# A sixth raw-weight buffer taken from the DMA scratch: one decoder layer in split float32 on one core

## The chip, the cores and the metric

The kernel runs on one core of one Trainium2 chip. The metric is device time in microseconds of one execution; three executions of the kernel before were timed, and the median counts. The profile is of one execution, taken by the hardware profiler.

## The reference

One decoder layer on 512 tokens of width 1024. Two token mixers run side by side on the normed input, are merged by sigmoid gates, and are followed by a squared-ReLU MLP.

```
h = rms_norm(x); proj = h @ w_in        # split into u, q, six key/value parts, gates
y_pool = pool_mixer(u)                  # causal means over 2, 4, 8, 16 tokens, then a small matmul
y_nsa  = nsa_mixer(q, kc, vc, ks, vs, kw, vw)   # compressed, selected and window attention, 16 heads
merged = g_a * (y_pool @ w_proj_pool) + g_b * (y_nsa @ w_proj_nsa)
x = x + merged @ w_out
x = x + square(relu(rms_norm(x) @ w_ff1)) @ w_ff2
return rms_norm(x)
```

All weights are float32 and each is read from HBM once or a few times.

## The kernel before, in words

**Weights.** Every matrix product is made of three products of split operands: a weight block of 128 x 1024 numbers (512 KB) is loaded into a raw tile, ScalarE copies it to a high part (`wh`), VectorE subtracts that from the raw block to get the low part (`wl`), and TensorE multiplies. One such pair of steps is called a conversion here. The blocks to be loaded stand in the list `LD`, in the order in which they are converted; `emit_load` (line 278) issues the next one on SyncE's queue (line 297). Before the change there are `RAW = 4` raw tiles, used in turn, so load number i has to wait until block i - 4 is converted. Four loads are issued at the start, and each conversion ends with one `emit_load`, so that in the program's order, too, loads run four conversions ahead.

**Converted parts.** They go into a ring of two places (`wh`, `wl`), or for the compression MLP and some gate blocks into one place called `wkt`. A block can only be converted when TensorE has finished with the one that had its place.

**Stages.** The stage up to attention ends at `N1` (number 37 in `LD`): compression keys (ck), selected keys (ks), the four pool groups (u0 to u3), the compression MLP (wk0 to wk3, wv0 to wv3), values (V0 to V2), the first queries (q0, q1, q2), the pool weights (wpool, number 19), and two groups of gate products in a seven-product Strassen form (A11, S3, S1 and so on; the first block of the first group is number 20). Then come attention, with the rest of the queries and gate columns as filler (`FILL2`), the NSA projection (pn0 to pn7), the output projection and the MLP, again in Strassen form. From `MLP0` (number 68) on tiles are handed back by name (`give_back`): `spare` collects them, and a seventh-product tile called raw5 joins there, so that five tiles are in use in the MLP.

**Sums of weights.** Some Strassen blocks are sums of two weight blocks. `make_sum` copies one block from HBM to HBM (tiles `S_g`, `S_o`, `S`; line 335, SyncE's queue), and `add_sum` adds the other with an accumulating DMA issued from GpSimd (line 343). Both are tied to the number of the load that has just been issued, and loads `raw<-S` read the result.

**Other traffic on SyncE's queue.** Each rotary embedding (`rope`) swaps halves with four small DMAs (line 882, `rs<-rx`, 64 KB each), on which VectorE's multiplications at line 899 wait.

**Order.** Instructions of an engine run in the order that a planner fixed when the program was built, from its own estimates of times; `tc.issue_after` (here `behind`) ties an instruction behind another of the same engine, and `tc.high_priority` moves one forward.

Of the kernel before, what the change touches and what calls it, by code (L numbers as in the profile page):

```python
# [62 lines left out]
def trunk(ctx: ExitStack, tc: tile.TileContext, A, out):  # L63
    nc = tc.nc
# [35 lines left out]
        return f[:, 1024 * i:1024 * i + 1024].rearrange("p (k t) -> p k t", k=4)  # L100

    WL, LD = [], []
    RAW = 4

    def add_w(key, ap):
        WL.append((key, len(LD)))
# [63 lines left out]
    for k in P1 + FILL2:  # L170
# [11 lines left out]
        if k == P1[-1]:  # L182
            N1 = len(LD)
# [85 lines left out]
    dest = {}  # L269

    raws, hls = {}, {}
    st = {"load": 0, "prep": 0, "use": 0, "kept": 0, "pairs": 0, "sums": 0}
    spare, slots_hl = [], []
    held, begun = {}, deque()

# [2 lines left out]
    def emit_load():  # L278

        i = st["load"]  # L280
        if i >= len(LD):
            return False
        segs = LD[i]
        a = segs[0][0].shape[1]
        b = sum(s.shape[2] for s, _ in segs)
        assert a * b <= 1024
        if not by_name() or st["kept"] < RAW:
            st["kept"] += by_name()
            t = wp.tile([128, 1024], F32, tag="raw", bufs=RAW, name=f"raw{i}")
        elif spare:  # L290
            t = spare.pop(0)
        else:
            return False
        st["load"] += 1
        v = t[:, :a * b].rearrange("p (a b) -> p a b", a=a)
        for s, o in segs:
            began[0] = nc.sync.dma_start(v[:, :, o:o + s.shape[2]], s)
        raws[i] = (t, a, b)
        for _ in range(sums_after(i)):
            make_sum(began[0])  # L300
        while i in EARLY[1:] and begun:
            add_sum()
        if (26 <= i < N1 and len(begun) > 1) or i >= N1 + len(FILL2) + 4 and (len(begun) > 2 or begun and st["sums"] == len(jobs)):
            add_sum()
        while i == MLP0 + 6 and len(begun) > 2:
            add_sum()
        return True
# [3 lines left out]
    def sums_after(i):  # L311

        if i < MLP0:
            return i in EARLY or i in (26, 27, 33, 35, 36) or N1 + 3 <= i < N1 + len(FILL2) or i == MLP0 - 2
        if i < MLP0 + 12:
            return {3: 1, 6: 4}.get(i - MLP0, 0)
        return (i - MLP0) % 3 == 0

    def by_name():

        return st["load"] >= MLP0

    def give_back(*tiles):
        spare.extend(tiles)
        while spare and by_name() and emit_load():
            pass

    def make_sum(load):

        if st["sums"] < len(jobs):  # L330
            to, q, _ = jobs[st["sums"]]
            while any(q is jobs[n][0] for n in begun):
                add_sum()
            with tc.issue_after(load.ins):
                nc.sync.dma_start(to, q)
            begun.append(st["sums"])
            st["sums"] += 1

    def add_sum(behind=None):

        to, _, q = jobs[begun.popleft()]
        with tc.issue_after(behind.ins) if behind else nullcontext():
            POOL.dma_start(to, q, accum_op=ALU.add)  # L343
# [28 lines left out]
    def group_steps(i):  # L372

        key, at = WL[i]
        if i in PLUS:
            while st["load"] <= PLUS[i]:
                assert emit_load()
            t = raws.pop(PLUS[i])[0]
            DVE.tensor_tensor(t, t, held[key], op=ALU.add)
            give_back(held.pop(key))  # L380
            yield
        elif isinstance(at, str):
            t = held.pop(key)
        else:
            while st["load"] <= at:
                assert emit_load()
            t = raws.pop(at)[0]
# [20 lines left out]
    kept = {}  # L408
# [52 lines left out]
    def wo_steps(i):  # L461
# [17 lines left out]
        if o in ("A12", "S2"):  # L479
# [3 lines left out]
            kept.pop("S2")  # L483
        if st["load"] > RAW + MLP0:
            give_back(t)
        else:
            emit_load()
            if st["kept"] == RAW:
                give_back()
# [4 lines left out]
    def emit_prep_half():  # L494
# [38 lines left out]
        raws.pop(at)  # L533
        if st["load"] > RAW + MLP0:
            give_back(t)
        else:
            emit_load()
            if st["kept"] == RAW:
                give_back()
# [246 lines left out]
    def behind(made):  # L786
        return tc.issue_after(made.ins)
# [22 lines left out]
    def evac0(i, after=None, root=None):  # L810
        sl = slice(128 * i, 128 * i + 128)
        for a in range(2):
            ks = slice(4 * a, 4 * a + 4)
            with behind(root) if root else nullcontext():
                r = ACT.activation(hT[0][:, ks, sl], trs[i][a], AF.Copy)
            with behind(after) if after else nullcontext():
                v = DVE.tensor_tensor(hT[1][:, ks, sl], trs[i][a], hT[0][:, ks, sl].bitcast(F32), op=ALU.subtract)
        for a in range(2 if i > 1 else 0):
            c = 128 * (i - 2)
            ACT.activation(quarter(MAf, 2 * a + 1)[:, :, c:c + 128], trs[i][a], AF.Copy)  # L820
        return r, v
# [7 lines left out]
    r, _ = evac0(1)  # L829
# [21 lines left out]
    made = []  # L851
# [5 lines left out]
        DVE.tensor_copy(identR, ident)  # L857
    c0.close()
    made0 = list(made)
    with behind(made[0]):  # L860
        ACT.activation(tick, rr[3][:, 1:2], AF.Sigmoid)

# [77 lines left out]
    with ExitStack() as c1:  # L940
# [254 lines left out]
        for k in P1[2:]:  # L1195
            i = int(k[-1]) if k[-1].isdigit() else None
# [533 lines left out]
    with ExitStack() as c3:  # L1730
# [21 lines left out]
        class Merged:  # L1752

            made = {b: [m[:, 4 * i:4 * i + 4, 256 * j:256 * j + 256] for m in mT]
                    for b, i, j in (("11", 0, 0), ("21", 1, 0), ("22", 1, 1))}
# [329 lines left out]
```

## Time and profile before

| what | value |
|---|---|
| three runs, us | 772.26, 770.54, 770.27 |
| median, us | 770.54 |
| profiled execution, span of the page, us | 767.4 |
| profiled execution's own time | not listed apart from its span; the median lies 3.1 us above the span |
| TensorE (PE) busy | 756.7 us, 99% |
| VectorE, ScalarE, GpSimd busy | 87%, 67%, 24% |
| mean busy share of the DMA engines by slice | from 0.1 to 1.0 |

The span runs from the first to the last instruction. Most executions of one kernel agree within 0.3%.

### The profile page before, as it was taken

How to read it: one execution, taken by the hardware profiler on the slowest of the kernel's cores; microseconds unless marked ns; L12 is line 12 of the kernel's file. 1: busy time of each engine (PE TensorE's matmuls, PEld its weight loads, DVE VectorE, ACT ScalarE, POOL GpSimd, SP SyncE). 2: the span in 40 equal slices, each digit the busy share in tenths (PEclk: the TensorE clock that was granted, in tenths of full speed). 3: DMA queues.
4: the chain of work that ended last, by engine and by line, in shares of the span. 5: the costliest groups of instructions: out<-in, count | busy, mean ns of one | idle time of the engine just before them, and what ended most of it. 6: DMA issues, size and time to landing. Idle time of an engine off the chain costs nothing.

```text
span 767.4 us, 13409 instructions
## 1 busy us (share of the span) xinstructions
PE 756.7 (99%) x4757; PEld 675.9 (88%) x4757; DVE 666.4 (87%) x1279; ACT 511.1 (67%) x977; POOL 184.2 (24%) x264
## 2 busy tenths in 40 slices
PE   9999999999999999999999999999999999999996
PEld 7889889888888888888889899989998999889985
DVE  7897999548988889989689689997989788978897
ACT  7766655328878888898745576954774477447754
POOL 4001010117746766574000200111111110111001
PEclk9999999999999999999999999999999999999999
DMA  9559993983051833371357965989998999799942
GB/s 308 165 143 266 251 230 108 257 214 115 15 176 52 158 56 70 56 138 60 116 186 220 324 111 185 287 219 299 310 259 222 314 303 257 215 325 294 293 171 110
DMA packets 119886, 150.76 MB, mean 196 GB/s; under 512 B 5782, under 2 KB 92346, under 8 KB 119611
## 3 DMA queue, kind: packets, MB, share of 16 engines
q1 hardware_dynamic: 98250, 122.90, 48.3%
q0 software_dynamic: 21280, 26.22, 22.8%
q8 instruction: 38, 0.62, 0.3%
q10 hardware_dynamic: 288, 0.79, 0.3%
q14 instruction: 30, 0.24, 0.1%
HBM read 145.16 MB, written 54.53 MB: 260 GB/s over the span
## 4 chain that ended last, share of the span: by engine, by line
PE 84%; DVE 9%; ACT 2%; DMA 2%; issue 1%; POOL 1%; SPq 0%; DVEq 0%; ACTq 0%; POOLq 0%
PE psB L638 20%; PE psB L1698 18%; PE psF L568 16%; PE psB L568 6%; PE psV L638 5%; PE psS L1378 4%; PE psT L1440 4%; PE psO L1474 4%; PE psB L1647 3%; DMA raw<-w_in 2%; PE psF L700 1%; DVE wl L527 1%; DVE PT L1456 1%; DVE P L1400 1%; DVE wkt L527 1%
## 5 line engine op out<-in xcount | busy, mean ns | idle before, releaser
L343 POOL DMA_DIRECT2D S<-w_ff x44 | 49.0, 1113 | 351.3 <-DMA S<-w_ff 290.3
L568 PE MATMUL psF<-R,wh 128*128 128x512 f32 x384 | 124.6, 400 | 0.0
L390 ACT ACTIVATE wh<-raw 128x1024 fp32r<-128x1024 f32 x73 | 77.1, 1058 | 70.0 <-PE psB L638 24.0
L1423 POOL TENSOR_SCALAR P<-P,sm,GT 128x128 f32<-128x128 f32 (+3 forms) x128 | 85.5, 724 | 68.8 <-DVE sm L1420 36.1
L395 DVE TENSOR_TENSOR wl<-raw,wh 128x1024 fp32r<-128x1024 f32 x73 | 88.9, 1219 | 12.7 <-ACT wh L390 12.2
L568 PEld LDWEIGHTS psF<-R,wh 128*128 128x128 f32 x384 | 68.8, 188 | 11.4 <-issue 0.2
L1410 ACT ACTIVATE P<-P,sm 128x128 f32<-128x128 f32 (+3 forms) x128 | 71.0, 557 | 9.9 <-DVE sm L1400 6.2
L568 PE MATMUL psF<-R,wl 128*128 128x512 f32 x192 | 75.5, 393 | 0.0
L524 ACT ACTIVATE wh<-raw 128x512 fp32r<-128x512 f32 (+1 forms) x76 | 45.1, 616 | 32.9 <-PE psF L568 21.2
L1400 DVE CUSTOM_DVE_ANT_0 P<-psS,cst 128x128 f32<-128x128 f32 (+3 forms) x128 | 59.3, 482 | 4.9 <-PE psT L1440 2.7
L390 ACT ACTIVATE w3h<-raw 128x1024 fp32r<-128x1024 f32 x37 | 39.2, 1059 | 34.0 <-PE psB L638 12.6
L527 DVE TENSOR_TENSOR wl<-raw,wh 128x512 fp32r<-128x512 f32 (+1 forms) x74 | 51.5, 707 | 9.2 <-ACT wh L524 8.9
L1451 ACT ACTIVATE PT<-psT 128x512 fp32r<-128x512 f32 (+2 forms) x96 | 49.0, 520 | 13.9 <-PE psT L1440 13.0
L1456 DVE TENSOR_TENSOR PT<-psT,PT 128x512 fp32r<-128x512 f32 (+2 forms) x96 | 56.2, 591 | 1.5 <-ACT PT L1451 1.3
L1440 PE MATMUL psT<-ident,P 128*128 128x128 f32 x320 | 50.1, 273 | 0.6 <-POOL rx L899 0.4
L395 DVE TENSOR_TENSOR w3l<-raw,w3h 128x1024 fp32r<-128x1024 f32 x37 | 45.1, 1220 | 4.7 <-ACT w3h L390 4.5
L1474 PE MATMUL psO<-PT,VV 128*128 128x256 f32 x320 | 48.5, 286 | 0.0
L1440 PEld LDWEIGHTS psT<-ident,P 128*128 128x128 f32 x320 | 39.6, 140 | 9.4 <-POOL rx L899 0.8
L638 PE MATMUL psB<-R,wh 128*128 128x256 f32 x336 | 46.3, 279 | 0.0
L1474 PEld LDWEIGHTS psO<-PT,VV 128*128 128x128 f32 x320 | 42.2, 188 | 1.3 <-ACT PT L1451 0.3
L638 PEld LDWEIGHTS psB<-R,wh 128*128 128x128 f32 x336 | 42.5, 188 | 0.2
L568 PEld LDWEIGHTS psF<-R,wl 128*128 128x128 f32 x192 | 36.0, 188 | 7.5
(442 smaller groups left out, 2083.7 us busy)
## 6 DMA issues: line engine op xcount, KB each, us to landing
raw<-w_ff SPq DMA_DIRECT2D x54, 512.0 KB, 6.2
S<-w_ff POOLq DMA_DIRECT2D x44, 512.0 KB, 8.2
raw<-S SPq DMA_DIRECT2D x44, 512.0 KB, 5.3
S<-w_ff SPq DMA_DIRECT2D x32, 512.0 KB, 7.3
raw<-w_in SPq DMA_DIRECT2D x31, 512.0 KB, 4.7
S<-S SPq DMA_DIRECT2D x12, 512.0 KB, 6.7
raw<-w_proj_nsa SPq DMA_DIRECT2D x8, 512.0 KB, 4.1
x<-x SPq DMA_DIRECT2D x7, 512.0 KB, 6.5
```

What stands on the lines that cost most here:

```text
L390: ACT.activation(h, t, AF.Copy)
L395: DVE.tensor_tensor(l, t, h.bitcast(F32), op=ALU.subtract)
L527: eng.tensor_tensor(l[:, sl], t[:, sl], h[:, sl].bitcast(F32), op=ALU.subtract)
L568: PE.matmul(ps, a, b, start=first and j == 0, stop=last and j == n - 1, skip_group_check=True)
L638: PE.matmul(out, w[u][:, k, 128 * f:128 * f + 128], moving[v][:, k, :], **kw)
L1400: DVE.tensor_tensor_reduce(out=P[:, o:o + n].rearrange("p (a c) -> p a c", c=128), in0=s, in1=m, scale=1.0, scalar=3e38, op0=ALU.add, op1= ...
L1410: last_exp[:] = [ACT.activation(c, c, AF.Exp, bias=sm[:, 0, e:e + 1], scale=-1.0, accum_out=sm[:, 1, e:e + 1])]
L1423: r = POOL.tensor_scalar(P[:, o:o + n], P[:, o:o + n], sm[:, 2, e:e + 1], GT[:, qb, c + e:c + e + 1], op0=ALU.mult, op1=ALU.mult)
L1440: PE.transpose(pt[:, 128 * j:128 * j + 128], P[:, 128 * j:128 * j + 128], ident)
L1456: return DVE.tensor_tensor(dL, src, dH.bitcast(F32), op=ALU.subtract)
L1474: PE.matmul(ps[:, qb % 2, :, :], VV[:, k, b, g, :], t[:, j, :, :], start=False, stop=last and j == len(kbs) - 1 and t is tL, skip_group_ch ...
L1698: PE.matmul(ps[f], self.Y.of(y)[u][:, 2 * g + k, 128 * f:128 * f + 128], w[v][:, k, :], start=first and g == k == u == v == 0, stop=g == k ...
```

## The change

The scratch that the DMA descriptors of GpSimd's queue use is set to 8192 bytes of each partition; the default is 16384. The 8 KB hold two more raw tiles of 4 KB. Two more loads are issued at the start of the first stage, so that loads run six conversions ahead; when number `N1` is reached, two turns of `emit_load` are passed over (`spared`), so that in the program's order loads run four ahead from there. The tiles stay six.

```diff
-    RAW = 4
+    RAW = 6
...
-    st = {"load": 0, "prep": 0, "use": 0, "kept": 0, "pairs": 0, "sums": 0}
+    st = {"load": 0, "prep": 0, "use": 0, "kept": 0, "pairs": 0, "sums": 0, "spared": 0}
...
+        if i == N1 and st["spared"] < 2:
+            st["spared"] += 1
+            return True
...
     made0 = list(made)
+    with behind(made[0]):
+        for _ in range(2):
+            emit_load()
...
-    nc = bacc.Bacc("TRN2", target_bir_lowering=False, num_devices=1)
+    nc = bacc.Bacc("TRN2", target_bir_lowering=False, num_devices=1, dynamic_dma_scratch_size=8192)
```

## Rows read from the trace of the kernel before

**Rows 1.** The page: busy time of each engine; the share of GpSimd's DMA queue.

```profile
PE 756.7 (99%) x4757; PEld 675.9 (88%) x4757; DVE 666.4 (87%) x1279; ACT 511.1 (67%) x977; POOL 184.2 (24%) x264
...
q0 software_dynamic: 21280, 26.22, 22.8%
```

**Rows 2.** Stretches: length; PE, PEld, DVE, ACT, POOL busy; PEclk, DMA share, GB/s.

```profile
0.00:20.00 20.00, 18.13 (x110) 14.29 (x111) 16.06 (x30) 14.93 (x28) 10.28 (x24) 1.00 0.98 309
20.00:160.00 140.00, 139.30 (x863) 125.38 (x862) 119.79 (x210) 81.80 (x140) 12.26 (x18) 1.00 0.79 202
160.00:360.00 200.00, 198.35 (x1260) 173.77 (x1259) 175.90 (x583) 165.23 (x447) 122.80 (x190) 1.00 0.41 94
360.00:440.00 80.00, 80.00 (x450) 69.95 (x449) 63.94 (x98) 45.49 (x76) 5.64 (x5) 1.00 0.68 215
440.00:768.00 328.00, 320.92 (x2081) 292.51 (x2079) 290.76 (x361) 203.62 (x289) 33.20 (x30) 0.99 0.87 245
```

**Rows 3.** Waits of PE: waited for, us in total, times, longest.

```profile
PE psZ L778 <- DVE zero L751: 1.1, 1, 1.1
PE psS L1378 <- DVE sm L1400: 0.8, 2, 0.5
PE psC L997 <- DVE wkt L527: 0.7, 1, 0.7
PE psT L1440 <- POOL rx L899: 0.4, 1, 0.4
PE psF L700 <- POOL wl L527: 0.3, 1, 0.3
```

**Rows 4.** Timeline, 84 to 89 us: start, duration, instruction, [idle before <- releaser].

```profile
86.75 0.68 DVE L527 TENSOR_TENSOR wkt<-raw,wkt 128x512 fp32r<-128x512 f32 x1
...
87.95 0.68 DVE L527 TENSOR_TENSOR wkt<-raw,wkt 128x512 fp32r<-128x512 f32 x1
...
88.69 0.30 PEld L997 LDWEIGHTS psC<-wkt,cA 128*128 128x128 f32 x2 [0.91 <-DVE wkt L527]
88.69 0.50 PE L997 MATMUL psC<-wkt,cA 128*128 128x256 f32 x2 [0.70 <-DVE wkt L527]
```

**Rows 5.** Timeline of ScalarE, then VectorE, 63 to 81 us.

```profile
75.24 0.73 ACT L524 ACTIVATE wpl<-raw 128x256 fp32r<-128x256 f32 x2 [3.19 <-DMA raw<-w_pool]
...
78.29 1.06 ACT L428 ACTIVATE wh<-raw 128x1024 fp32r<-128x1024 f32 x1 [0.43 <-DMA raw<-w_in]
...
63.43 0.85 DVE L527 TENSOR_TENSOR wl<-raw,wh 128x304 fp32r<-128x304 f32 x2
...
67.01 1.29 DVE L527 TENSOR_TENSOR wl<-raw,wh 128x512 fp32r<-128x512 f32 x2 [1.35 <-ACT wh L524]
...
75.69 0.76 DVE L527 TENSOR_TENSOR wpl<-raw,wpl 128x256 fp32r<-128x256 f32 x2 [2.02 <-ACT wpl L524]
...
79.39 1.23 DVE L431 TENSOR_TENSOR wl<-raw,wh 128x1024 fp32r<-128x1024 f32 x1
```

**Rows 6.** Timeline of SyncE's queue: wpool's load and the first gate block's.

```profile
68.33 0.37 SPq L297 DMA_DIRECT2D raw<-w_pool  x1
...
72.90 0.38 SPq L297 DMA_DIRECT2D raw<-w_in  x1
```

**Rows 7.** The page: issues by line, KB each, median us to landing.

```profile
raw<-w_pool SPq DMA_DIRECT2D x1, 256.0 KB, 6.9
```

**Rows 8.** Line 343, GpSimd's accumulating DMAs, and the last line of that answer.

```profile
L343 POOL DMA_DIRECT2D S<-w_ff x44: 1028/1150/1274, 143.3 to 720.8; - x44
...
DMA to landing us min/median/max: 6.1/8.2/12.4
```

**Rows 9.** Line 882, the swaps of the rotary embedding: time to landing, whole span.

```profile
DMA to landing us min/median/max: 1.9/2.0/4.9
```

**Rows 10.** Waits over the whole span, of ScalarE and of SyncE's queue.

```profile
ACT W1H L524 <- DMA raw<-w_out: 6.1, 3, 3.6
...
SPq L297 <- DVE w3l L395: 75.5, 24, 28.3
```

## The prediction

> **What bounds the kernel now.** I read the page's busy line first: TensorE (PE) is busy for 756.7 of 767.4 us and no other engine for more than 87% [rows 1]. The five stretches then say where the 10.7 us without PE lie [rows 2]. The start has 20 - 18.13 = 1.87 us, the first stage 140 - 139.30 = 0.70, attention 200 - 198.35 = 1.65, the projections nothing, and the last stretch 328 - 320.92 = 7.08, of which 0.56 lies behind the end of the span (768 - 767.44) and the rest behind the last matmul. The granted clock is 1.00, so 2.4 GHz, in all but the last stretch, where the drained tail brings it to 0.99; the change adds no PE work and touches no clock. PE's list of waits says the same by name [rows 3]: 1.1 us at the very start, 0.7 in the compression MLP, 0.8 and 0.4 in attention, 0.3 for the first low part, and three more of 0.2 (the list has eight entries). Together 3.9 us. No entry names a DMA. What a change to the loads can win is thus small, and must come through an engine that PE waits for.
>
> One wait of PE does lead back to loads: the 0.7 us of `psC` for the low part of `wkt` (the compression MLP's last block, wv3). In the timeline PE starts again at 88.69 after 0.70 us, its weight loads after 0.91 us, when VectorE ends the second half at 87.95 + 0.68 = 88.63 [rows 4]. VectorE reached it late: from 79.39, the first gate block's low part, it works without a gap to 88.63, after standing idle earlier for 2.02 us behind ScalarE, which itself stood idle 3.19 us for the load of wpool and 0.43 us for the first gate block [rows 5]. Those two loads are what the change moves.
>
> **Two more tiles in the first stage: part one of the sum.** With four tiles, load 19 (wpool) takes the tile of block 15 (u3). VectorE ends that conversion at 67.01 + 1.29 = 68.30 [rows 5], and the load is issued at 68.33 and takes 6.9 us [rows 6, 7]. With six it takes the tile of block 13 (V2), whose low part ends at 63.43 + 0.85 = 64.28 [rows 5]: 4.0 us sooner. At the same 6.9 us it lands near 71.2. ScalarE got to it at 75.24 - 3.19 = 72.05, so the whole 3.19 us goes. Load 20, the first gate block, was issued at 72.90 [rows 6]; its new tile is that of block 14, long converted, so it follows right behind load 19 and lands before 76. Its conversion at 78.29 is then no longer tied to the load. It is next tied to its place in the ring, which PE frees when it ends u3's products, and that is earlier than 78.29 by about 2 us, by the order of the program (an estimate: two blocks, u3 and q0, hold the two places).
>
> VectorE's gapless run of 88.63 - 79.39 = 9.24 us then starts up to 2.02 us sooner, and the low part that PE waits for is ready near 86.6, before PE wants it at 88.69 - 0.70 = 87.99. PE's wait goes: 0.70 us by its own row, 0.91 by its weight loads. I take 0.9, because products behind that wait can't start before their weight load. PE is without a gap from there into attention but for tenths, so what is won here is kept.
>
> **The rest, at nothing, and what hides it.** The two extra loads at the start are SyncE's instructions (`behind(made[0])` ties only instructions of ScalarE, whose instruction made[0] is). They cost SyncE 0.4 us each, as any issue does [rows 6], on a queue that has waits in it. The cover is the fresh tile: loads 4 and 5 wait for no conversion now. Without it they would land when they do today. Sums that hang on the number of a load are copied two conversions sooner; the DMA share of the first stage is 0.79 [rows 2], so there is room on average. In attention the program's order is four ahead as before, but tile by tile the loads may run up to two conversions sooner; the DMA share is 0.41 there and no engine's wait on a load shows in PE. In the projections ScalarE waits 6.1 us for `w_out` [rows 10] and PE not at all: cover of PE's queue, worth nothing if it goes. In the MLP seven tiles are in use where five were; SyncE's longest wait for one, 28.3 us [rows 10], becomes shorter, and PE has no wait there to lose. If this cover were gone, the price would be a late load of up to 6.9 us, the row of wpool.
>
> **The halved scratch.** It is used by GpSimd's queue alone: 50 accumulating DMAs, 44 of them in the MLP's blocks, each 1.15 us of GpSimd's time at the median and 8.2 us to landing [rows 8], 21280 packets in all [rows 1], so 426 each and 27 on each of 16 engines. Lower bound of the cost: nothing. Upper bound: if only one transfer found room at a time, each would wait up to 8.2 us for the one ahead; where four are issued within some 5 us, the last would come three landings later, about 3 x (8.2 - 1.2) = 21 us. Its reader has far more lead than that in most places, as the 28.3 us of waiting show, so I bound the loss at 8 us. I take nothing, because 27 packets of a transfer are few.
>
> The Trainium skill has a rule that speaks against this edit: Debugging Trainium Hangs, section 4 (Descriptor Overflow), names too many descriptors for the carveout of 16 KiB per partition on GpSimd's queue as a cause of trouble, and DMA: Bandwidth & Descriptors (Terms) gives a descriptor as 16 B. By these figures, as an estimate, 8 KiB would hold 512 descriptors, some 19 transfers of 27; the sum by it is the one above, and no row here shows a full ring.
>
> **Sum.** 767.4 - 0.9 = 766.5 us of span, and with the 3.1 us by which the median of the runs lies above the profiled span, 769.6 us. A measurement of this kernel can tell about 0.3%, 2.3 us, from no change.
>
> **Rivals.**
>
> *The wait stays (0.17).* VectorE's order is fixed by the planner. If pool mixing and gate conversions only close up in front of the same wait, or the planner puts the freed time elsewhere, PE waits as before: 770.5. For it: VectorE is busy 119.79 of 140 us in this stage [rows 2]. Against it: its idle 2.02 us lie right ahead of the run.
>
> *More goes (0.10).* A new order also takes away attention's named waits, 0.8 + 0.4 + two of 0.2, and the 0.3 + 0.2 of the start: 0.9 + 1.6 + 0.5 = 3.0, so 767.5. Against it: none of them names a load.
>
> *Slower, by a swap behind a load (0.13).* SyncE issues the swaps of the rotary embedding on the queue of the loads. They land after 2.0 us at the median and 4.9 at most [rows 9]. With more loads in flight, a swap that now takes 2.0 takes 4.9; VectorE, in order, stands at line 899 for 2.9 us, behind it the conversions and then PE: 770.5 + 2.9 = 773.4. It decides where VectorE has less than 2.9 us of lead over PE. For it: the 0.91 us wait shows a place without lead. Against it: the 4.9 us swap of today gave PE no wait that its list has.
>
> The Trainium skill's rule for it (DMA: Bandwidth & Descriptors, Two DMAs through the same engine are not ordered) is that descriptors of one queue start in order on a DMA engine, so a small transfer stands behind a large one ahead of it; the 4.9 us agree with that.
>
> *Slower, by a full scratch (0.02).* Accumulating DMAs wait for room, at most 8 us by the bound above: up to 778.5. It decides if a reader's load is then issued after its conversion's turn.
>
> **How the numbers follow.** The forecast, the wait gone and tenths elsewhere, has the chance 0.58, with its own range of 768.6 to 770.6. The first rival lies inside it or close to it. Together they hold 0.75; to leave out no more than 0.2 the range goes down to the case of more, with a little room, 767.2, and up to where the swap rival's partial waits lie, 772.8. Faster by over 0.3%, below 768.2: most of the third case, and a share of the first where small waits go too, 0.17. Slower by over 0.3%, above 772.8: the last two cases, 0.14 with their rounding. Within: 0.69.
>
> **What would show it.** Right: wpool's load issued near 64, no ScalarE wait for it; no wait of PE for `wkt` near 88; PE busy close to 140 of 140 us in the first stage; GpSimd's accumulating DMAs as long as now; the MLP's PE time unchanged. Wrong: a wait of VectorE at line 899, PE waits above 1.65 us in attention, or GpSimd's 1.15 us growing. The forecast fails if the planner's new order costs attention more than the first stage wins.

## The result and the profile after

The changed kernel takes 775.68 us (median of 5 runs, 774.76 to 776.01) against 770.27 us for the kernel before in the same comparison (5 runs, 769.57 to 772.26): ratio 1.0066, 95% interval 1.0052 to 1.0079. It is 5.4 us slower. The profiled executions agree: 773.3 us of span against 767.4. In the changed kernel's file most lines named here stand 3 further down, those from about 860 on 6.

The five stretches of the changed kernel, with the columns of [rows 2]:

```profile
0.00:20.00 20.00, 17.76 (x108) 14.10 (x109) 15.39 (x30) 14.39 (x28) 10.53 (x27) 1.00 0.99 304
20.00:160.00 140.00, 140.00 (x870) 126.51 (x870) 120.23 (x210) 82.22 (x140) 12.78 (x15) 1.00 0.87 223
160.00:360.00 200.00, 198.17 (x1258) 173.48 (x1257) 177.21 (x584) 165.76 (x448) 122.36 (x189) 1.00 0.38 85
360.00:440.00 80.00, 76.54 (x420) 65.84 (x419) 60.70 (x94) 43.11 (x71) 7.26 (x7) 0.98 0.88 243
440.00:768.00 328.00, 326.77 (x2109) 297.38 (x2107) 292.28 (x363) 203.84 (x291) 31.08 (x28) 1.00 0.81 231
```

The first stage did what was forecast: PE is busy for 140.00 of 140 us, where it missed 0.70 [rows 2]. Attention has almost the busy time of before (198.17 for 198.35). The loss is in the fourth stretch, which PE filled before (80.00) and now leaves empty for 3.46 us, at a granted clock of 0.98 and with a DMA share of 0.88 instead of 0.68. The last stretch only inherits the delay: the work that ended at 767.4 us now ends at 773.3.

The first stage in single rows of the changed kernel: wpool on SyncE's queue [rows 6],

```profile
58.67 0.37 SPq L300 DMA_DIRECT2D raw<-w_pool  x1
```

and on ScalarE [rows 5],

```profile
65.18 0.73 ACT L527 ACTIVATE wpl<-raw 128x256 fp32r<-128x256 f32 x2 [0.70 <-DMA raw<-w_pool]
```

GpSimd's accumulating DMAs with their landing [rows 8],

```profile
L346 POOL DMA_DIRECT2D S<-w_ff x44: 1032/1146/1241, 129.4 to 720.7; - x44
...
DMA to landing us min/median/max: 6.1/8.6/12.4
```

and the landing of the swaps [rows 9]:

```profile
DMA to landing us min/median/max: 1.9/2.0/5.9
```

wpool is issued 9.7 us sooner (58.67 for 68.33) and ScalarE waits 0.70 us for it instead of 3.19. GpSimd issues its accumulating DMAs in the same time.

PE's list of waits in the changed kernel (waited for, us in total, times, longest):

```profile
PE psB L1653 <- DVE wl L477: 2.4, 1, 2.4
...
PE psB L571 <- DVE wl L530: 1.0, 2, 0.7
PE psS L1384 <- DVE sm L1406: 1.0, 3, 0.5
```

The wait for `wkt` of [rows 3] is gone. New are 2.4 and 1.0 us for low parts in the projections (`psB`, lines 1653 and 571). PE names VectorE, but VectorE had been late since 383 us. The chain that ended last shows behind whom (start, length, piece):

```profile
373.53 8.91 DMA raw<-w_out
...
382.46 0.64 ACT W1H L527
```

ScalarE's waits from 360 to 425 us give the size. Before, it waited three times for `w_out`, 6.1 us in all and 3.6 at the longest [rows 10]; in the changed kernel:

```profile
ACT W1H L527 <- DMA raw<-w_out: 10.1, 3, 6.5
...
ACT w3h L474 <- DMA raw<-S_o: 4.9, 1, 4.9
```

The wait for `S_o` follows from the one for `w_out`: in the same chain that load is asked for at 386.90, behind the low part of the late block, and lands 4.24 us later.

The load of `w_out` that ScalarE stands for was asked for at the same time in both kernels, 373.54 and 373.53 us. It then took 3.8 us before and takes 8.9 now. The next two fences list the DMAs issued from 372.5 to 374.5 us (KB each, median us from issue to landing), the kernel before first.

```profile
raw<-w_out SPq DMA_DIRECT2D x1, 512.0 KB, 3.8
```

```profile
S<-w_ff POOLq DMA_DIRECT2D x1, 512.0 KB, 11.1
raw<-w_out SPq DMA_DIRECT2D x1, 512.0 KB, 8.9
```

What is beside it stands on the queues. SyncE's queue at the end of attention, before:

```profile
360.44 0.53 SPq L297 DMA_DIRECT2D raw<-S  x1
...
373.54 0.38 SPq L297 DMA_DIRECT2D raw<-w_out  x1
```

In the changed kernel:

```profile
359.89 0.52 SPq L300 DMA_DIRECT2D raw<-S  x1
360.54 0.50 SPq L338 DMA_DIRECT2D S<-S  x1
...
361.71 1.24 SPq L338 DMA_DIRECT2D S<-w_ff  x2
373.53 0.38 SPq L300 DMA_DIRECT2D raw<-w_out  x1
```

And GpSimd there:

```profile
367.04 1.18 POOL L346 DMA_DIRECT2D S<-w_ff  x1 [6.49 <-DMA S<-S]
370.28 1.06 POOL L346 DMA_DIRECT2D S<-w_ff  x1 [2.06 <-DMA S<-w_ff]
371.55 1.03 POOL L346 DMA_DIRECT2D S<-w_ff  x1 [0.21 <-issue]
```

Three copies of weight sums (issued from 360.54 to 362.3 us, the last landing at 371.0) and their three accumulating DMAs (landing at 375.8, 378.7 and 382.7 us) now run here. In the kernel before the copies started at 429.77 us. (The fourth sum of that load is built from another sum, and its copy comes only at 414.59 us in the changed kernel.) The reason is a number. `raw5`, the tile that attention frees, goes to whichever MLP load comes to it first (`raw<-S` at 360 us in both). With four tiles in turn the fifth MLP load (MLP0 + 4) took it, and no sum hangs on that. With six, loads MLP0 + 4 and MLP0 + 5 have tiles in turn, and the seventh (MLP0 + 6) takes `raw5`; `sums_after`, the function that ties sums to load numbers, hangs four sums on exactly that one.

### The profile page after: what moved, and what is told of

It reads as the page before. It is cut to its first block, busy times and chain, and to the rows that moved or that the text cites. A ratio compares the mean times of both kernels' runs of the same rounds, so it can differ in the third digit from the quotient of the medians.

```text
span 773.3 us, 13406 instructions
## 1 busy us (share of the span) xinstructions
PE 759.2 (98%) x4757; PEld 677.3 (88%) x4757; DVE 666.9 (86%) x1279; ACT 510.0 (66%) x977; POOL 184.0 (24%) x264
## 3 DMA queue, kind: packets, MB, share of 16 engines
q1 hardware_dynamic: 98250, 122.90, 48.8%
q0 software_dynamic: 21280, 26.22, 22.5%
## 4 chain that ended last, share of the span: by engine, by line
PE 85%; DVE 8%; ACT 3%; DMA 2%; issue 1%; POOL 0%; POOLq 0%; DVEq 0%; ACTq 0%; SPq 0%
PE psB L641 20%; PE psF L571 18%; PE psB L1704 18%; PE psV L641 5%; PE psB L571 4%; PE psS L1384 4%; PE psT L1446 4%; PE psO L1480 3%; PE psB L1653 2%; PE psV L571 2%; PE psF L703 2%; DMA raw<-w_out 1%; DVE P L1406 1%; DVE PT L1462 1%; PE psC L1003 1%
```

## The experiments

**1. Sums on the next load.** The changed kernel, otherwise untouched.

```diff
-        while i == MLP0 + 6 and len(begun) > 2:
+        while i == MLP0 + 7 and len(begun) > 2:
...
-            return {3: 1, 6: 4}.get(i - MLP0, 0)
+            return {3: 1, 7: 4}.get(i - MLP0, 0)
```

> The changed kernel, with its four sums hung on the MLP's eighth load instead of its seventh. Theory (the sums' copies and GpSimd's accumulating transfers now run at 360 to 372 us because the seventh load takes the raw tile that attention frees; they hold back w_out's transfer, 8.9 us instead of 3.8, and all queued behind ScalarE's wait for it): the copies move behind the projections, w_out's transfer is back near 4 us, TensorE is busy for about 80.0 of the 80 us from 360 instead of 76.5, and the time is 768.5 to 770, that is 0.997 to 1.000 of the time before, since the first stage's 1 us is kept. Rivals (the planner's new order on ScalarE, the halved scratch, or the fullness of seven raw tiles in the MLP): the stretch keeps its 76.5 and the time stays at 775 to 776, ratio 1.0066.

Measured: 769.61 us, ratio 0.9994 (0.9985 to 1.0003), span 767.8. Its issue of `w_out` and its fourth stretch:

```profile
raw<-w_out SPq DMA_DIRECT2D x1, 512.0 KB, 3.5
```

```profile
360.00:440.00 80.00, 79.68 (x446) 69.10 (x445) 63.13 (x97) 44.69 (x73) 6.31 (x7) 1.00 0.71 220
```

One number in two lines takes the whole loss away. The scratch, the six tiles, the seven tiles in the MLP and the planner's other choices are all still there, so none of them by itself is its cause. The first stage's gain was kept in that stage, but not to the end: the time is that of before.

**2. The scratch alone.** The kernel before, with one argument added.

```diff
+    nc = bacc.Bacc("TRN2", target_bir_lowering=False, num_devices=1, dynamic_dma_scratch_size=8192)
```

> The kernel before with the halved scratch alone, no other edit. Theory (the scratch costs nothing): 770.3 us, ratio 0.999 to 1.001, GpSimd's accumulating transfers issued in the same 1.1 us each. Rival (the smaller scratch holds GpSimd's transfers back): they are issued later or land later, and the time goes toward 775.

Measured: 769.48 us, ratio 0.9993 (0.9983 to 1.0004). The accumulating DMAs of its line 343 [rows 8]:

```profile
L343 POOL DMA_DIRECT2D S<-w_ff x44: 1028/1152/1277, 142.7 to 721.6; - x44
...
DMA to landing us min/median/max: 6.0/8.4/12.6
```

The halved scratch costs nothing that can be measured.

**3. Only four tiles in turn from the MLP on.**

```diff
-    RAW = 6
+    RAW, KEEP = 6, 4
...
-        if not by_name() or st["kept"] < RAW:
+        if not by_name() or st["kept"] < KEEP:
```

(and `KEEP` for `RAW` in the four places where tiles are given back)

> The changed kernel, with six raw tiles up to the end of attention but only four of them kept in the rotation from there, so that the raw tile that attention frees goes to the MLP's fifth load again and the seventh load with its four sums comes later. Theory of the sums' place: the copies are back behind 400 us, TensorE's stretch from 360 is full again, and the time is 768.5 to 770. Rival (the seven tiles of the MLP themselves cost time): the time also falls to about 770, so this run alone doesn't tell those two apart; with the sums moved alone it does. Rival (halved scratch, or the order of the first stage): it stays at 775.

Measured: 769.60 us, ratio 0.9993 (0.9984 to 1.0001). The fifth MLP load gets `raw5` again, the sums move back, and PE is busy for 79.71 of 80 us in the fourth stretch. Either way of moving the sums gives the same time.

**4. The same sums put early in the kernel before.** Four tiles, full scratch.

```diff
-        while i == MLP0 + 6 and len(begun) > 2:
+        while i == MLP0 + 4 and len(begun) > 2:
...
-            return {3: 1, 6: 4}.get(i - MLP0, 0)
+            return {3: 1, 4: 4}.get(i - MLP0, 0)
```

> The kernel before, with its four tiles and full scratch, and the four sums hung on the MLP's fifth load, the one that takes the raw tile that attention frees. Theory (the sums' transfers at the end of attention are by themselves enough): the copies run from about 360 us, w_out lands late, by some 3 to 5 us, TensorE loses 3 to 6 us in the 80 us from 360, and the time is 773.5 to 776, ratio 1.004 to 1.0075. Rivals (six tiles, the planner's order or the scratch are needed for the loss): 770 to 771, ratio within 0.001 of one.

Measured: 774.91 us, ratio 1.0066 (1.0050 to 1.0083). Its issues from 372.5 to 374.5 us and its fourth stretch:

```profile
S<-w_ff POOLq DMA_DIRECT2D x2, 512.0 KB, 9.9
raw<-w_out SPq DMA_DIRECT2D x1, 512.0 KB, 10.3
```

```profile
360.00:440.00 80.00, 76.99 (x431) 66.56 (x430) 59.47 (x91) 41.31 (x68) 7.00 (x6) 1.00 0.80 224
```

The sums at that place are by themselves enough to slow down the kernel before, with nothing of the change in it. With run 1 this settles what made the time longer. That the ratio is the same to four digits is chance: followed through the same matmuls, run 4 loses 4.0 us between 373 and 430 us and another 1.4 between 430 and 500, where the changed kernel loses 5.9 and then nothing more.

**5 to 7. Copies or accumulating DMAs?** Run 5 keeps the copies of the changed kernel and takes accumulating DMAs away, run 6 leaves one sum of the four at the early place, run 7 takes the accumulating DMAs of all four away. Runs 5 and 7 thus leave sums half made and compute something else; only their times are of use. In this order their edits are:

```diff
         while i == MLP0 + 6 and len(begun) > 2:
-            add_sum()
+            begun.popleft()
```

```diff
-        while i == MLP0 + 6 and len(begun) > 2:
+        while i in (MLP0 + 6, MLP0 + 7) and len(begun) > 2:
...
-            return {3: 1, 6: 4}.get(i - MLP0, 0)
+            return {3: 1, 6: 1, 7: 3}.get(i - MLP0, 0)
```

```diff
-        while i == MLP0 + 6 and len(begun) > 2:
-            add_sum()
+        while i == MLP0 + 6 and begun:
+            begun.popleft()
```

> The changed kernel, with the sums' copies still hung on the MLP's seventh load, but the accumulating transfers of two of the three left out and the third put off to a later load (two sums thus stay half made, and their products are wrong). In the changed kernel the copies run from 360.5 to 371.0 us and the accumulating transfers from 367.0 to 382.6, so w_out's transfer, asked for at 373.5, has only the latter beside it. Theory A (the accumulating transfers hold w_out back): w_out lands after about 4 us, TensorE is full from 360 to 440 but for the 0.3 to 0.6 us that the run with later sums lost too, and the time is 769 to 770. Theory B (the copies are enough): w_out stays near 8 us and the time at 774 or more.

> The changed kernel, with one sum on the MLP's seventh load and three on its eighth. Theory (the price is traffic that comes together with w_out's transfer): one copy and one accumulating transfer, done before about 376 us, a third of the traffic and mostly ahead of w_out; w_out lands some 1 to 2 us late at most, and the time is 769.5 to 771. Rival (any accumulating transfer at that place delays the projections by the full amount): 774 to 776.

> The changed kernel with the sums' copies where they are, and the accumulating transfers of these four sums all left out (the four sums stay half made, and their products are wrong). With the third transfer still running at 370.9 to 377.5 us the run before it had w_out land after 7.1 us. Theory (an accumulating transfer in flight beside w_out is what holds it back): none runs here, w_out lands after about 4 us, TensorE loses at most 0.3 to 0.8 us from 360 to 440, and the time is 769 to 770. Rival (the copies delay the projections, in whatever way): w_out stays at 7 us or above, and the time at 772.5 to 775.

Run 5 measured 772.97 us, ratio 1.0038 (1.0022 to 1.0054), between the two theories. The expectation had put the third accumulating DMA off to a later load, but it wasn't put off. GpSimd had stood idle for 10.85 us and issued the DMA when its copy had landed, whatever load it is written behind. GpSimd in run 5, then its `w_out`:

```profile
370.89 1.08 POOL L346 DMA_DIRECT2D S<-w_ff  x1 [10.85 <-DMA S<-w_ff]
```

```profile
raw<-w_out SPq DMA_DIRECT2D x1, 512.0 KB, 7.1
```

Run 6 measured 769.62 us, ratio 0.9998 (0.9987 to 1.0008). It has one accumulating DMA as well, but a sooner one, which landed at 373.89 us; `w_out` was asked for at 373.62:

```profile
367.34 1.18 POOL L346 DMA_DIRECT2D S<-w_ff  x1 [6.69 <-DMA S<-S]
```

```profile
raw<-w_out SPq DMA_DIRECT2D x1, 512.0 KB, 3.8
```

Run 7 measured 769.73 us, ratio 1.0005 (0.9993 to 1.0017), `w_out` in 3.8 us, and its fourth stretch is:

```profile
360.00:440.00 80.00, 78.86 (x440) 68.27 (x439) 62.81 (x96) 44.78 (x73) 2.49 (x3) 1.00 0.70 217
```

So the price follows the number of accumulating DMAs that are in flight while `w_out` is:

| run | beside `w_out` | `w_out`, us | ratio |
|---|---|---|---|
| sums later (1) | none | 3.5 | 0.9994 |
| one sum early (6) | one, landing as it starts | 3.8 | 0.9998 |
| copies only (7) | none | 3.8 | 1.0005 |
| one accumulating DMA (5) | one | 7.1 | 1.0038 |
| changed kernel | three | 8.9 | 1.0066 |
| sums early in before (4) | three | 10.3 | 1.0066 |

The copies had landed by 371 us in runs 5 and 7 and in the changed kernel and don't delay `w_out`. Run 7 still lost 1.14 us in the stretch, some 0.8 more than run 1. That is one stall: PE stands 0.82 us at 408.85 for a low part of line 477. Shortly before, at 401.72, ScalarE ended a wait of 1.21 us for a later load of `w_out`, which took 5.0 us where run 1's took 4.0 and ScalarE waited 0.21. Why that load is slower stays open.

**8. Without the two turns passed over.**

```diff
-        if i == N1 and st["spared"] < 2:
-            st["spared"] += 1
-            return True
```

> The changed kernel without the two turns passed over, so that loads are six conversions ahead in the program's order everywhere. Theory (a load's time is set by its tile's last conversion, six back, in both, so the passing over moves no transfer by much): the same loss at the projections and 774.5 to 776.5. Rival (the passing over is what puts the seventh load, and with it the sums, at the end of attention): the sums move, and the time falls to about 770, or the loss moves elsewhere.

Measured: 777.31 us, ratio 1.0098 (1.0075 to 1.0122), above the range given. The main point held: the three accumulating DMAs are where they were and `w_out` takes 9.5 us. The passing over is not what brought the sums forward. Leaving it out costs about 2.2 us more by the profiled spans (775.5 and 773.3), some 0.7 of it idle in attention (PE busy 197.50 of 200 us) and 1.1 in the fourth stretch (75.44 of 80). Why stays open.

**9. Keeping the lead.** Run 1 brought PE out of attention 0.6 us early and had lost 0.5 of that by the projections. ScalarE in run 1:

```profile
369.44 0.62 ACT L527 ACTIVATE W1H<-raw 128x512 fp32r<-128x512 f32 x1
370.08 1.28 ACT L1749 ACT_TABLE_LOAD   x1
...
371.49 2.18 ACT L527 ACTIVATE wh<-raw 128x512 fp32r<-128x512 f32 x4
```

The first block of `w_out` is there two conversions sooner than before, so the planner put its conversion ahead of the table load; `wh`, which PE waits for, comes 0.62 us later than it could. The edit, on top of run 1 (`seen` holds each block's conversion):

```diff
-                conv[0] = ACT.activation(h[:, sl], t[:, sl], AF.Copy)
+                with tc.issue_after(seen["pn3"].ins) if WL[i][0] == "wo10" else nullcontext():
+                    conv[0] = ACT.activation(h[:, sl], t[:, sl], AF.Copy)
+                seen[WL[i][0]] = conv[0]
```

> The run with later sums, and besides ScalarE's first conversion of w_out put behind that of pn3. With later sums alone TensorE came out of attention 0.6 us early and gave that back at 372 us, where ScalarE's conversion for w_out (369.44, 0.62 us) stands ahead of the table load and of wh. Theory (this conversion alone takes the lead back): TensorE doesn't stand at 372 us, and the profiled span is 0.6 us shorter, 767.2, with a time of 768.8 to 769.4, ratio 0.998 to 0.9995. Rival (TensorE waits for wh's raw tile or VectorE there anyway): no change from the run with later sums, 769.6.

Measured: 768.80 us, ratio 0.9986 (0.9976 to 0.9996), span 767.4. ScalarE in this run:

```profile
369.40 1.28 ACT L1751 ACT_TABLE_LOAD   x1
...
370.81 1.14 ACT L528 ACTIVATE wh<-raw 128x512 fp32r<-128x512 f32 x2
```

`wh` is 0.68 us sooner, and PE no longer starts late at 372 us. By the medians this version beats the kernel before by about 1 us, which is below the 0.3% that the prediction counted as no change. One execution doesn't show it: the profiled spans are equal, 767.4. In this trace PE is 0.8 us ahead of the kernel before from 362 to 408 us and 0.25 at the end; between, it stands 0.28 us at 414.72 for VectorE (line 1799), as in run 1. So only a part of what the first stage wins is shown to reach the end.

## Why the prediction was wrong

**The same work in both traces.** Matmuls that stand at the same place of the program start, in us:

| where | before | after | after - before |
|---|---|---|---|
| first stage, ahead of the wait for `wkt` | 77.59 | 77.85 | +0.26 |
| first stage, behind it | 118.64 | 117.62 | -1.02 |
| attention | 243.07 | 242.09 | -0.98 |
| attention, later | 297.97 | 297.44 | -0.53 |
| end of attention | 360.68 | 360.14 | -0.54 |
| projections | 373.76 | 373.76 | 0.00 |
| projections | 388.04 | 389.29 | +1.25 |
| projections | 402.32 | 404.21 | +1.89 |
| behind the stall at 412 | 430.19 | 436.05 | +5.86 |
| MLP | 498.30 | 504.16 | +5.86 |

**The first stage: right in what it wins, wrong in the tile.** ScalarE's wait shrank, VectorE's late run closed up, and PE's wait for `wkt` went. The term was 0.9 us. The stretch shows 0.70, all the idle time that it had; the same matmuls win 1.28, of which 1.06 at the wait for `wkt`. But wpool's load was to be issued near 64, behind block 13 (V2), and came at 58.67. V2's low part ended no sooner (64.44 for 64.28). In the trace the tiles go round in the order in which conversions end: wv0, block 14, ends at 55.07, ahead of V1, block 12, at 58.64. So load 18 follows wv0 (55.13), load 19, wpool, follows V1, and V2's tile goes to load 20 (64.47). The rule of the text before the prediction, that load i waits for block i - 4, holds in the kernel before only where the order is that of the numbers: there too load 16 follows wv0 (55.97 behind 55.94) and not V1 (59.04).

**Kept up to the projections: half right.** Of the 1.0 us ahead, 0.45 go at 244 us, in attention. VectorE's addition of a rotary embedding takes 0.90 us there instead of 0.41, and PE then waits for VectorE (`psS`, line 1384). VectorE first before, then after:

```profile
241.43 0.41 DVE L892 TENSOR_TENSOR rx<-rx,rs 128x256 f32<-128x256 f32 x1
```

```profile
240.45 0.90 DVE L898 TENSOR_TENSOR rx<-rx,rs 128x256 f32<-128x256 f32 x1
```

All eight kernels with six tiles have the long addition (0.89 to 0.91) and the three with four have the short one (0.41 to 0.42). GpSimd works beside it with six tiles (line 1429, 239.03 to 241.08 us in the changed kernel) and had ended before it with four (240.07 in the kernel before). In the whole trace of the kernel before, the 11 of these 20 additions beside which GpSimd stood idle took 0.40 to 0.42 us, the others up to 0.83. So GpSimd's work is the likely reason; no run isolates it. PE's idle time in attention came to 1.83 us, above the 1.65 that the prediction gave as a sign of being wrong. The 0.54 us that were left went at 372 us. Run 9 showed where: one conversion ahead of a table load. The prediction held that what was won would be kept, as PE had no gap there. But PE without a gap can still have no slack: `wh` was ready when PE came to it, and no sooner.

**The failed step: "Sums that hang on the number of a load are copied two conversions sooner; ... there is room on average".** Two things in it were wrong. The sums of load MLP0 + 6 moved by some 70 us, not by two conversions, because the sixth tile changed which load takes `raw5`. The text before the prediction names `raw5` as the tile that joins the rotation, and the code ties four sums to one number; taking loads from 68 on in turn through six tiles would have shown it. And the room was judged by a mean over the first stage, for sums that ran at the end of attention. The DMA share of the changed kernel's 362 to 382 us is 1.03 and 1.08:

```profile
362.00:372.00 10.00, 10.00 (x54) 8.39 (x51) 4.35 (x8) 9.91 (x17) 2.69 (x3) 1.00 1.03 309
372.00:382.00 10.00, 9.98 (x43) 7.80 (x43) 6.38 (x11) 3.41 (x7) 0.58 (x1) 1.00 1.08 228
```

In the kernel before the same two windows have 0.38 and 0.45.

**"ScalarE waits 6.1 us for `w_out` [rows 10] and PE not at all: cover of PE's queue, worth nothing if it goes".** This was read in one direction only. A load on which an engine already stands has no cover of its own: `w_out` came 5.1 us later, ScalarE's longest wait for it grew from 3.6 to 6.5 us, and PE, behind ScalarE and VectorE, lost 5.9 us between 373 and 430 us. The price named for a gone cover, a load late by up to 6.9 us, had the right size, though it stands beside the MLP's tiles; it was given no rival and no chance.

**The sum, as it came out.** From 0.54 us ahead at 360 to 5.86 behind at 436, PE lost 6.4 us. The table has them at four places: 0.54 are the late start at 372; 1.25 and 0.64 go near 385 and 396 for low parts of line 530; 3.97 are the stall of 2.42 us for the low part of line 477 and the clock behind it, 1.5, below. For the two low parts PE's list of waits has 1.0 us, since the ends of matmuls are modelled; the weight loads in front of them have 1.9:

```profile
PEld psB L571 <- DVE wl L530: 1.9, 2, 1.1
```

The 3.1 us that the prediction added to the span were too many: a run's time lies some 1.8 us above its own span (775.07 and 773.3), so the profiled execution of the kernel before took some 769.2 us, an estimate, and was quicker than the median.

**The halved scratch: right, at nothing.** The full scratch as a rival is out by run 2. The overflow that the Trainium skill warns of (Debugging Trainium Hangs, section 4, Descriptor Overflow) shows in none of the runs at 8 KB; transfers land after 8.1 to 8.7 us at the median in these runs, where they landed after 8.2.

**The swap as the slower rival: wrong mechanism.** The slowest swap now lands after 5.9 us instead of 4.9, but it is issued at 49.98, in the first stage, where PE has no gap. In attention the slowest takes 4.4 instead of 4.2, and line 899 runs on GpSimd there, not on VectorE. The sign and a part of the size that this rival foresaw came from elsewhere, so they are luck.

## What to carry to other kernels

Where side transfers are hung on the number of a load, a change in the number of buffers moves them: before judging such a change, follow the turn of the buffers through every point at which the pool changes, and list what is tied to the loads whose turn jumps. Judge room for them in the 10 us in which they will run, and look there for an engine that already waits for a load: that is the place without slack, even if the bounding engine shows no wait. In this kernel the tiles went round in the order in which they came free, which was not that of the loads' numbers. And an early load can hurt by the order it lets a planner choose; look at what the conversion is now put ahead of.

## What was not expected of the hardware

**Accumulating DMAs weigh more than their bytes.** A plain 512 KB load in the same window took 3.5 to 3.8 us, and 7.1 with a single accumulating DMA of 512 KB issued 2.1 us ahead of it. In run 7 the three copies of the same size were out of the way by the time of `w_out`. A copy beside a load is found near 397 us, where in several runs one of 512 KB is issued 0.4 us behind a load of `w_out`; the load then took 4.0 us in run 1 and 5.0 in run 7 (issues from 396.9 to 397.4 us in run 1, from 396.6 to 397.1 in run 7):

```profile
raw<-w_out SPq DMA_DIRECT2D x1, 512.0 KB, 4.0
```

```profile
raw<-w_out SPq DMA_DIRECT2D x1, 512.0 KB, 5.0
```

Here the load goes first and in run 5 the accumulating DMA did, so this is no clean comparison. The page of the kernel before points the same way as a mean over the span: the queue of loads, swaps and copies takes 48.3% of the 16 engines' span for 122.90 MB, GpSimd's 22.8% for 26.22 MB [rows 1], 2.2 times as much time for a byte.

```profile
q1 hardware_dynamic: 98250, 122.90, 48.3%
```

**A stall of PE took some of its clock with it.** Two windows of the changed kernel, columns as in [rows 2], and PE's timeline around them:

```profile
410.00:413.00 3.00, 0.58 (x5) 0.38 (x4) 3.00 (x4) 1.75 (x3) 0.00 (x0) 1.00 1.04 151
413.00:417.00 4.00, 4.00 (x23) 4.00 (x23) 4.00 (x8) 2.21 (x3) 0.00 (x0) 0.57 0.88 275
```

```profile
412.73 0.38 PE L1653 MATMUL psB<-wl,R 128*128 128x256 f32 x1 [2.42 <-DVE wl L477]
...
413.33 0.41 PE L1653 MATMUL psB<-wl,R 128*128 128x256 f32 x1
413.54 0.41 PE L1653 MATMUL psB<-wh,R 128*128 128x256 f32 x1
```

After 2.42 us without work the granted clock is 0.57 over the next 4 us, so at the lower level of 1.2 GHz for most of them; sixteen matmuls start 0.21 us apart instead of 0.12, which adds 1.5 us to the stall. Runs 5 and 8, each with a stall of 2.6 us, show the same (0.58 and 0.57). Run 4, whose longest stall was 1.4 us, keeps a clock of 1.00 there. The prediction held that the change touches no clock; through this stall it did.
